# Feed-forwards ordered by a planner in the kernel, and a fourth quad in four gate/up blocks of each

## The chip, the cores and the metric

The kernel runs on one core of a Trainium2 chip. The metric is device time in microseconds (us) of one execution. TensorE is PE in the profile, its weight loads are PEld, VectorE is DVE, ScalarE is ACT, GpSimd is POOL, and SyncE is SP, which here only issues DMAs.

## What is computed

One block of a network over 256 tokens of width 2048: a gated feed-forward, a mixer (a recurrent branch and a pooling branch), and a second feed-forward, each behind a norm, with a norm on its result and a residual sum.

```python
D_MODEL, SEQ, D_FF = 2048, 256, 5632

def _swiglu(x, w_gate, w_up, w_down):
    return (jax.nn.silu(x @ w_gate) * (x @ w_up)) @ w_down

f = _swiglu(_rmsnorm(h, ln_ffn1_pre), ffn1_gate, ffn1_up, ffn1_down)
h = h + 0.5 * _rmsnorm(f, ln_ffn1_post)
mx = _hybrid_mixer(_rmsnorm(h, ln_mix_pre), w_in, ..., w_out)
h = h + _rmsnorm(mx, ln_mix_post)
f = _swiglu(_rmsnorm(h, ln_ffn2_pre), ffn2_gate, ffn2_up, ffn2_down)
h = h + 0.5 * _rmsnorm(f, ln_ffn2_post)
```

All inputs and the output are float32.

## The kernel before

**Products.** Every float32 operand is split into a high half, rounded to the type `F32R` that TensorE multiplies, and a low half, the rest. A product is three matmuls (`mm3`, lines 177 to 179): high times high, high times low, low times high. Activations lie transposed and split, 128 rows of k by 256 tokens; "h" is one of the two halves of 128 tokens. Weights come from memory in pieces of 128 rows of k (a k-tile) by 512 columns; ScalarE writes the high half and VectorE subtracts it from the raw weight to get the low half (lines 153 and 154 for plain pieces, 392 and 393 inside a quad). The split weights lie in a ring of `WS_BUFS` = 5 buffers of 1024 columns, the raw ones in `W32_BUFS` = 4. A pool of `NUNITS` = 33 buffers ("units") of 1024 columns holds everything longer-lived.

**Stages of a feed-forward.** Gate and up are made in eleven blocks of 512 columns over the 16 k-tiles; block 0 runs under another order, block 1 is plain, blocks 2 to 10 (`FAST`) go through `seven`. The result of a block is transposed in squares on VectorE, moved by 16 DMAs that POOL issues (`carry_at`, line 635), and split again (lines 647 and 651). Then the down projection runs over 44 k-tiles as two calls of `seven` with 1024 columns each (`post`), with a norm and the residual at the end; the last 16 k-tiles run one token half after the other (`by_half`). The mixer's out projection goes through `post` as well.

**Pairs and quads.** `seven` makes two column blocks at once (f and l: gate and up, or two neighbours of the down projection). A `pair` takes two k-tiles of one column block: four products, 12 matmuls. A `quad` takes two k-tiles of both column blocks and does with seven products (21 matmuls) what pairs do with eight. It needs sums of weights (`t13`, line 377; `t2`, line 381; `t4`, line 385), four splits (lines 392, 393), and sums of activations, which `sums` makes once per feed-forward (lines 268 to 317). Its partial products stand in banks of their own and are put together in `merge` (lines 416 and 419); `total` (line 435) adds what belongs to the second column block; lines 720, 724 and 623 are the gate's nonlinearity, the product and the transposition. A call with `n` quads takes 2n k-tiles out of both column blocks. Gate/up blocks have `NG` = 3 quads, after the third and fifth f pair and the second l pair (`SPOTS`).

**Order.** TensorE, ScalarE and VectorE run in the order in which the program emits their instructions. That order comes from a list of TensorE's work (`put`, each with its length) and events (`at`), which run when the sum of these lengths passes a time that is written by hand or taken from the ring (`slot`). SP and POOL are ordered by the framework's own scheduler.

Of the kernel before, what the change touches and what calls it, by code (L numbers as in the profile page):

```python
# [11 lines left out]
F32 = mybir.dt.float32  # L12
# [6 lines left out]
P = 128  # L19
# [23 lines left out]
AHEAD = (5.0, 6.0)  # L43
# [12 lines left out]
ROWS2 = [("r_k", 8), ("gn_w", 8), ("gn_b", 8), ("pool_scale", 8)]  # L56


class Block:
    def __init__(s, tc, ctx):  # L60
# [5 lines left out]
        s.late, s.after, s.items, s.events, s.now = [], [], deque(), [], 0.0  # L66
        s.clk, s.uses = 0.0, []
# [35 lines left out]
    def at(s, t, fn):  # L103

        s.n += 1
        heapq.heappush(s.events, (t, s.n, fn))

    def slot(s, end):

        s.uses.append(end)  # L110
        n = len(s.uses) - 1 - WS_BUFS
        return s.uses[n] if n >= 0 else n - 1.0

    def run(s):

        s.now = 0.0
        E = mybir.EngineType
        with s.tc.manual_schedule(engines={E.PE, E.Activation, E.DVE}):
            while s.items or s.events:
                while s.events and (s.events[0][0] <= s.now or not s.items):  # L120
                    heapq.heappop(s.events)[2]()
                if s.items:
                    t, fn = s.items.popleft()
                    fn()
                    s.now += t
            s.stats()
        s.now = s.clk = 0.0
        s.uses = []

    def put(s, t, fn):  # L130
        s.items.append((t, fn))
        s.clk += t
# [48 lines left out]
    def gemm_tok(s, w, c0, at, KT, evac, lead=False, trail=False, xs=None, hold=False,  # L181
# [19 lines left out]
        if trail:  # L201
            both(0, KT - TRAIL)
            s.by_half(w, c0, KT - TRAIL, KT, s.clk, AHEAD[0], do, keep,
                      lambda h: evac(h, pss[h]))
            return
        k0 = 0
        if xs:
            s.head(w, c0, KT, do, keep, xs)
            k0 = KT
        elif lead:  # L210
            s.by_half(w, c0, 0, STAG, s.clk, AHEAD[1], do, keep)
            s.run()
            k0 = STAG
        both(k0, KT)
        if hold:
            for h in range(2):
                s.at(0.3 + 1.6 * h, lambda h=h: evac(h, pss[h]))
            return
# [4 lines left out]
    def gemm_at(s, w, c0, at, KT, evac):  # L223

        pss = []
        ws = {}

        def load(k):
            ws.update((i, (wH, wL)) for i, wH, wL in s.load_w(w, k, 2, c0, 512))

        def do(k):
            if not pss:
                pss.extend(s.pm.tile([P, 512], F32, tag="mm", name=s.nm("mm"))
                           for _ in range(2))
            for h in range(2):
                (wH, wL), (xH, xL) = ws[k], at(k)
                s.mm3(pss[h], xH[:, h * P:h * P + P], xL[:, h * P:h * P + P], wH, wL,
                      k == 0, k == KT - 1)
        for k in range(0, KT, 2):
            s.at(s.slot(s.clk + 12 * MM), lambda k=k: load(k))  # L240
            s.put(6 * MM, lambda k=k: do(k))
            s.put(6 * MM, lambda k=k: do(k + 1))
        for h in range(2):
            s.at(s.clk + 0.3 + 1.6 * h, lambda h=h: evac(h, pss[h]))

    def by_half(s, w, c0, k0, k1, start, ahead, do, keep, done=None):

        for k in range(k0, k1, 2):
            s.at(start + (k - k0) * 3 * MM - ahead,
                 lambda k=k: keep(s.load_w(w, k, 2, c0, 512, k - k0 >= STAG)))  # L250
        for h in range(2):
            for k in range(k0, k1):
                s.put(3 * MM, lambda k=k, h=h: do(k, h))
            if done:
                s.put(0, lambda h=h: done(h))

    def sums(s, T, out, when, own=None, nq=2):

        nc = s.nc
        V = nc.vector  # L260
        tt = {}
        fl = lambda t: t.rearrange("p a b t -> p (a b t)")

        def first():
            xH, xL = [t[:, :2 * nq].bitcast(F32).rearrange("p k t -> p (k t)")
                      for t in T[len(out) // 2]]
# [15 lines left out]
        def parts():  # L282

            j = len(out) // 2
# [14 lines left out]
        def lows():  # L299
# [3 lines left out]
            for i in range(2):  # L303
                out.append([(s12[0][:, m, i], s12[1][:, m, i]) for m in range(2)]
                           + [tuple(u[:, i] for u in v) for v in (s3, s4)])
# [9 lines left out]
        def fourth():  # L315
            f, fH, fL = tt["f"], tt["H"], tt["L"]
            V.tensor_tensor(out=fl(fL), in0=fl(f), in1=fl(fH).bitcast(F32), op=ALU.subtract)
            for i in range(nq):
                out.append([(fH[:, m, i], fL[:, m, i]) for m in range(4)])
        for i, fn in enumerate((first, second) + ((parts, lows) if own is not None  # L320
                                                  else (third, fourth))):
            s.at(when + 1.7 * i, fn)

    def seven(s, wf, cf, wl, cl, at, KT, T, sm, n, spots, ev_first, ev_last, trail=0,
              one_end=False, ends=(-0.05, 2.7)):


        nc = s.nc
        V = nc.vector
        K0 = 2 * n  # L330

        bank = {}
        std = KT - K0
        left = dict(f0=std + n, f1=std, l0=std + n, l1=std + n, p1=n, p5=n, p6=n, p7=n)

# [16 lines left out]
        def pair(k, w, c0, b):  # L352
            s.at(s.slot(s.clk + 12 * MM), lambda: keep(s.load_w(w, k, 2, c0, 512)))
# [5 lines left out]
            s.put(12 * MM, do)  # L359

        def quad(q):
            k = 2 * q
            v, x = {}, {}
            a, b, c, d = [s.slot(s.clk + m * MM) for m in (6, 9, 15, 21)]

            def get():
                va, vb = [s.wp.tile([P, 1024], F32, tag="w32", name=s.nm("w32"),
                                    bufs=W32_BUFS).rearrange("p (a c) -> p a c", a=2)
                          for _ in range(2)]
                for dst, kk, w, c0 in ((va[:, 0], k, wl, cl), (vb[:, 0], k, wf, cf),  # L370
                                       (va[:, 1], k + 1, wf, cf), (vb[:, 1], k + 1, wl, cl)):
                    nc.sync.dma_start(out=dst, in_=w[kk * P:kk * P + P, c0:c0 + 512])
                v.update(a=va, b=vb[:, 1:], t13=s.unit((P, 2, 512), F32, "t13"),
                         t24=s.unit((P, 2, 512), F32, "t24"), b0=vb[:, :1])

            def t13():
                V.tensor_tensor(out=v["t13"], in0=v["a"],  # L377
                                in1=v["b0"].to_broadcast([P, 2, 512]), op=ALU.subtract)

            def t2():  # L380
                V.tensor_tensor(out=v["t24"][:, 0], in0=v["a"][:, 0], in1=v["t13"][:, 1],  # L381
                                op=ALU.add)

            def t4():
                V.tensor_tensor(out=v["t24"][:, 1], in0=v["b"][:, 0], in1=v["t24"][:, 0],  # L385
                                op=ALU.subtract)

            def split(n_, m):
                wH = s.wp.tile([P, 1024], F32R, tag="wH", name=s.nm("wH"), bufs=WS_BUFS)
                wL = s.wp.tile([P, 1024], F32R, tag="wL", name=s.nm("wL"), bufs=WS_BUFS)  # L390
                H, L = [t_[:, :m * 512].rearrange("p (a c) -> p a c", a=m) for t_ in (wH, wL)]
                nc.scalar.copy(H, v[n_])  # L392
                V.tensor_tensor(out=L, in0=v[n_], in1=H.bitcast(F32), op=ALU.subtract)  # L393
# [6 lines left out]
            s.put(6 * MM, lambda: (mul("p1", rows(k, 0), x["a"][0]),  # L400
                                   mul("f0", S_(4), x["a"][1])))
            s.put(3 * MM, lambda: mul("l0", rows(k + 1, 0), x["b"][0]))
            s.put(6 * MM, lambda: (mul("p5", S_(1), x["t13"][0]),
                                   mul("p7", S_(3), x["t13"][1])))
            s.put(6 * MM, lambda: (mul("p6", S_(2), x["t24"][0]),
                                   mul("l1", rows(k + 1, 1), x["t24"][1])))
        u = []

        gap = 0.1 if one_end else 1.4

        def merge():
            m = s.clk

            def start():
                u.extend(s.tmp("u") for _ in range(4))
                nc.scalar.copy(u[0], bank["p1"])

            def add(o, b, i):
                V.tensor_tensor(out=u[o], in0=bank[b], in1=u[i], op=ALU.add)  # L419
            s.merged = m + 0.7  # L420
# [1184 lines left out]
```

## Time and profile before

| | us |
|---|---|
| median of 3 runs | 2030.01 |
| lowest and highest of the runs | 2029.83, 2030.64 |
| profiled execution: span from its first to its last instruction | 2028.3 |
| PE busy | 2012.7 (99%) |
| DVE busy | 1746.8 (86%) |
| ACT busy | 1159.4 (57%) |
| mean granted TensorE clock | 0.998 |

The profile is of one execution; the page gives its span and no time of its own besides, so the runs stand beside it. A matmul's record is its latency, so TensorE's busy time says that it worked, not how densely. In a row of a timeline stand the start, the length, the engine, the line, the operation, the tiles that it writes and reads, the shapes, the count of merged neighbours and, in brackets, idle time before it with what ended it. In a row of waits stand who waited for whom, the total in us, how often, and the longest.

### The profile page before, as it was taken

How to read it: one execution, taken by the hardware profiler on the slowest of the kernel's cores; microseconds unless marked ns; L12 is line 12 of the kernel's file. 1: busy time of each engine (PE TensorE's matmuls, PEld its weight loads, DVE VectorE, ACT ScalarE, POOL GpSimd, SP SyncE). 2: the span in 40 equal slices, each digit the busy share in tenths (PEclk: the TensorE clock that was granted, in tenths of full speed). 3: DMA queues.
4: the chain of work that ended last, by engine and by line, in shares of the span. 5: the costliest groups of instructions: out<-in, count | busy, mean ns of one | idle time of the engine just before them, and what ended most of it. 6: DMA issues, size and time to landing. Idle time of an engine off the chain costs nothing.

```text
span 2028.3 us, 28794 instructions
## 1 busy us (share of the span) xinstructions
PE 2012.7 (99%) x10011; PEld 1664.0 (82%) x10011; DVE 1746.8 (86%) x2304; ACT 1159.4 (57%) x1559; POOL 323.4 (16%) x673
## 2 busy tenths in 40 slices
PE   9999999999999999999999999999999999999997
PEld 7888888888888888888788788888888888888886
DVE  6999999999998867799689577869999999999986
ACT  7555555555555566685576444565555555555553
POOL 0122111221000023413220111001211112110000
PEclk9999999999999999999999999999999999999999
DMA  7667676676667777757556558676676767666674
GB/s 261 192 207 224 218 219 207 209 222 213 197 218 258 224 213 211 203 177 215 148 171 186 160 169 274 206 220 193 202 226 211 227 200 227 217 208 203 213 258 146
DMA packets 226841, 423.55 MB, mean 209 GB/s; under 512 B 24063, under 2 KB 27529, under 8 KB 226697
## 3 DMA queue, kind: packets, MB, share of 16 engines
q1 hardware_dynamic: 204137, 384.70, 61.1%
q0 software_dynamic: 22272, 36.51, 5.5%
q8 instruction: 78, 1.28, 0.3%
q10 hardware_dynamic: 288, 0.52, 0.1%
q14 instruction: 66, 0.54, 0.1%
HBM read 396.69 MB, written 8.39 MB: 200 GB/s over the span
## 4 chain that ended last, share of the span: by engine, by line
PE 97%; issue 1%; DVE 1%; ACT 0%; POOL 0%; DMA 0%; POOLq 0%; DVEq 0%; SPq 0%; ACTq 0%
PE mm L177 27%; PE mm L179 27%; PE mm L178 27%; PE ms L177 4%; PE ms L178 4%; PE ms L179 4%; PE tr L605 1%; PE pA L1326 0%; PE mc L576 0%; PE pU L1422 0%; DMA w<-in_ffn_gate_dram 0%; PE pSa L1434 0%; PE pY L1457 0%; PE pT L1493 0%; PE pM L1392 0%
## 5 line engine op out<-in xcount | busy, mean ns | idle before, releaser
L177 PE MATMUL mm<-wH,xH 128*128 128x512 f32 (+1 forms) x2232 | 870.4, 391 | 0.0
L179 PE MATMUL mm<-wH,xL 128*128 128x512 f32 (+1 forms) x2232 | 866.2, 388 | 0.7 <-DVE xL L613 0.7
L178 PE MATMUL mm<-wL,xH 128*128 128x512 f32 (+1 forms) x2232 | 866.1, 388 | 0.0
L154 DVE TENSOR_TENSOR wL<-w,wH 128x1024 fp32r<-128x1024 f32 (+2 forms) x551 | 660.4, 1211 | 183.3 <-ACT wH L153 175.4
L153 ACT CAST wH<-w 128x1024 fp32r<-128x1024 f32 (+2 forms) x551 | 567.3, 1045 | 351.5 <-PE mm L179 241.9
L179 PEld LDWEIGHTS mm<-wH,xL 128*128 128x128 f32 x2232 | 419.0, 188 | 87.9 <-DVE xL L613 1.5
L177 PEld LDWEIGHTS mm<-wH,xH 128*128 128x128 f32 x2232 | 418.9, 188 | 86.9 <-issue 0.4
L178 PEld LDWEIGHTS mm<-wL,xH 128*128 128x128 f32 x2232 | 419.2, 188 | 83.9 <-DVE wL L154 0.3
L392 ACT CAST wH<-t 128x1024 fp32r<-128x1024 f32 x172 | 181.0, 1054 | 283.8 <-DVE t L385 180.0
L635 POOL DMA_DIRECT2D x<-T x352 | 172.3, 498 | 734.0 <-issue 401.1
L393 DVE TENSOR_TENSOR wL<-t,wH 128x1024 fp32r<-128x1024 f32 x172 | 209.9, 1223 | 11.1 <-ACT wH L392 6.6
L393 DVE TENSOR_TENSOR wL<-w,wH 128x1024 fp32r<-128x1024 f32 (+1 forms) x172 | 163.6, 951 | 1.1 <-ACT wH L392 1.1
L392 ACT CAST wH<-w 128x1024 fp32r<-128x1024 f32 (+1 forms) x172 | 140.4, 832 | 25.6 <-DMA w<-in_ffn_down_dram 13.5
L377 DVE TENSOR_TENSOR t<-w,w 128x1024 f32<-128x1024 f32 x86 | 105.0, 1220 | 2.3 <-DMA w<-in_ffn_down_dram 2.3
L179 PE MATMUL ms<-wH,sL 128*128 128x512 f32 x174 | 67.7, 389 | 0.0
L178 PE MATMUL ms<-wL,sH 128*128 128x512 f32 x174 | 67.7, 389 | 0.0
L177 PE MATMUL ms<-wH,sH 128*128 128x512 f32 x174 | 67.7, 389 | 0.0
L419 DVE TENSOR_TENSOR u<-ms,u 128x512 f32<-128x512 f32 x92 | 61.4, 687 | 1.4
L688 POOL DMA_DIRECT2D R<-R x96 | 47.0, 497 | 84.1 <-issue 72.2
L385 DVE TENSOR_TENSOR t<-w,t 128x512 f32<-128x512 f32 x86 | 59.1, 687 | 0.0
L381 DVE TENSOR_TENSOR t<-w,t 128x512 f32<-128x512 f32 x86 | 59.1, 687 | 0.0
L814 POOL DMA_DIRECT2D gb<-in_ln_ffn_post_dram x4 | 2.2, 557 | 285.0 <-PE mm L179 142.6
(323 smaller groups left out, 1986.1 us busy)
## 6 DMA issues: line engine op xcount, KB each, us to landing
w<-in_w_in_dram SPq DMA_DIRECT2D x128, 512.0 KB
w<-in_ffn_up_dram SPq DMA_DIRECT2D x122, 512.0 KB
w<-in_ffn_gate_dram SPq DMA_DIRECT2D x120, 512.0 KB
w<-in_ffn_down_dram SPq DMA_DIRECT2D x116, 512.0 KB
w<-in_ffn_down_dram SPq DMA_DIRECT2D x120, 256.0 KB
w<-in_ffn_gate_dram SPq DMA_DIRECT2D x112, 256.0 KB
w<-in_ffn_up_dram SPq DMA_DIRECT2D x108, 256.0 KB
w<-in_w_out_dram SPq DMA_DIRECT2D x28, 512.0 KB
```

The source lines that it names most:

```text
L153: s.nc.scalar.copy(vH, v)
L154: s.nc.vector.tensor_tensor(out=vL, in0=v, in1=vH.bitcast(F32), op=ALU.subtract)
L177: nc.tensor.matmul(ps, aH, bH, start=start, stop=False)
L178: nc.tensor.matmul(ps, aH, bL, start=False, stop=False)
L179: nc.tensor.matmul(ps, aL, bH, start=False, stop=stop)
L377: V.tensor_tensor(out=v["t13"], in0=v["a"], in1=v["b0"].to_broadcast([P, 2, 512]), op=ALU.subtract)
L381: V.tensor_tensor(out=v["t24"][:, 0], in0=v["a"][:, 0], in1=v["t13"][:, 1], op=ALU.add)
L385: V.tensor_tensor(out=v["t24"][:, 1], in0=v["b"][:, 0], in1=v["t24"][:, 0], op=ALU.subtract)
L392: nc.scalar.copy(H, v[n_])
L393: V.tensor_tensor(out=L, in0=v[n_], in1=H.bitcast(F32), op=ALU.subtract)
L419: V.tensor_tensor(out=u[o], in0=bank[b], in1=u[i], op=ALU.add)
L635: nc.gpsimd.dma_start(out=x[0][q * 32:q * 32 + 32, i], in_=src[i * 32:i * 32 + 32, q])
```

## The change

The hand-set times go. `Plan` collects every operation of the feed-forwards and of `post` as a node: engine, duration (`cost`), what it depends on, which buffers it takes and gives back, and for TensorE its place in time. `solve` derives due times backward from TensorE's places, then runs the list forward: at each step the engine whose next operation can start first gets the one that is due first. The program is emitted in that order; SP is now ordered by it too. A raw weight may take a unit where its four buffers are full. The order of pairs and quads is written as strings, in which f and l are pairs and q a quad. Blocks 3, 5, 7 and 9 have four quads; the other strings repeat the patterns of before. The activation sums for the third and fourth quad are made together (`SUMS`).

```diff
-AHEAD = (5.0, 6.0)
-DOWN = ((0, 7, ((8, 12), (0, 3, 5, 7, 9)), 0),
-        (2, 8, ((2, 4, 6, 8, 10, 12), (0, 2)), TRAIL))
-OUT = ((0, 0, (), 0), (1, 2, ((4,), (0,)), 0), (3, 0, (), TRAIL))
-FAST = range(2, 11)
-CARRY = (18, 21)
-NG, SPOTS = 3, ((2, 4), (1,))
+DOWN = ((0, "fffffffffqffffqff" "lqlllqllqllqllqlllll", 0),
+        (2, "fffqffqffqffqffqffqf" "lqllqlll", TRAIL))
+OUT = ((0, "", 0), (1, "fffffqf" "lqlllll", 0), (3, "", TRAIL))
+GATE_UP = ["", "ffffffffllllllll"] + ["fffqffqllqlll", "ffqfqfqlqlll"] * 4 + ["fffqffqllqlll"]
+SUMS = (2, 2)
+LAT = dict(PE=0.22, DVE=0.1, ACT=0.17, SP=0.0, POOL=8.0)
+UNITS = dict(ffn=25, out=22)
+FIFO = dict(pt=4, pm=4, tmp=TB)
+SPARE, KEEP, URGENT = 3, 4, 8.0
+SOON, LATEST, BEFORE = 22.0, 12.0, 12.0
+EARLY = 0.5
+RATE, LEAVE, LAND = 0.25, 1.05, 2.0
...
+def cost(eng, n, extra=0.0):
+    return extra + (n / 960 + 0.068 if eng == "DVE" else n / 1200 + 0.095)
...
+    def solve(s):
...
+        for n in reversed(s.nodes):
+            for m in succ[n]:
+                if n.eng == "PE":
+                    break
+                v = m.due - n.dur - (n.lat + (EARLY if m.eng == "PE" else 0.0)
+                                     if m.eng != n.eng else 0.0)
+                n.due = v if n.due is None else min(n.due, v)
+            if n.due is None:
+                n.due = n.born + LATEST
...
+        while len(order) < len(s.nodes):
+            best = None
+            for e, c in front.items():
+                got = [(when(n), n) for n in c]
+                if got:
+                    first = min(a for a, _ in got)
+                    a, n = min((x for x in got if x[0] <= first + 1e-9),
+                               key=lambda x: x[1].due)
+                    if best is None or a < best[0]:
+                        best = (a, n)
...
+            if n.size:
+                line = max(n.free + LEAVE, line) + n.size / RATE
+                n.end = max(n.end, line + LAND)
...
     def run(s):
...
-        with s.tc.manual_schedule(engines={E.PE, E.Activation, E.DVE}):
-            while s.items or s.events:
...
+        with s.tc.manual_schedule(engines={E.PE, E.Activation, E.DVE, E.SP}):
+            for n in s.plan.solve():
+                n.fn()
             s.stats()
...
+    def fetch(s, w, k, c0, keep, hold=False):
+
+        p, x = s.plan, {}
+        src = Tok("w32", "unit")
+        dst = [Tok("unit"), Tok("unit")] if hold else [Tok("ring")]
...
+        n = p.op("SP", 0.4, load, take=[src], size=0.52, chain="SP")
+        n = p.op("ACT", cost("ACT", 1024), cast, [n], take=dst, chain="cast")
+        return p.op("DVE", cost("DVE", 1024), low, [n], rel=[src]), dst
...
         def quad(q):
...
-            for t, fn in ((a, get), (a, t13), (a, lambda: split("a", 2)), (a, t2),
-                          (b, lambda: split("b", 1)), (b, t4), (c, lambda: split("t13", 2)),
-                          (d, lambda: split("t24", 2))):
-                s.at(t, fn)
...
+            ld = [p.op("SP", 0.4, lambda m=m: get(m), take=([ka], [kb], (), ())[m], size=0.26,
+                       chain="SP") for m in range(4)]
...
+            one, two = cost("DVE", 512), cost("DVE", 1024)
+            n13 = p.op("DVE", two, t13, ld[:3], [k13, k24], [ka, kb])
+            la, ra = half("a", 2, [ld[0], ld[2]], [ka])
+            n2 = p.op("DVE", one, t2, [n13], (), [ka, k13])
+            lb, rb = half("b", 1, [ld[3]], [kb])
+            n4 = p.op("DVE", one, t4, [n2, ld[3]], (), [kb])
+            l13, r13 = half("t13", 2, [n13], [k13])
+            l24, r24 = half("t24", 2, [n4], [k24])
...
+            p.pe(6 * MM, lambda: (mul("p1", rows(k, 0), x["a"][0]),
+                                  mul("f0", S_(4), x["a"][1])),
+                 [la, ds, dep(k)] + claim("p1", "f0", "f1"), ra)
+            p.pe(3 * MM, lambda: mul("l0", rows(k + 1, 0), x["b"][0]),
+                 [lb] + claim("l0", "l1"), rb)
+            p.pe(6 * MM, lambda: (mul("p5", S_(1), x["t13"][0]),
+                                  mul("p7", S_(3), x["t13"][1])),
+                 [l13] + claim("p5", "p7"), r13)
+            d = p.pe(6 * MM, lambda: (mul("p6", S_(2), x["t24"][0]),
+                                      mul("l1", rows(k + 1, 1), x["t24"][1])),
+                     [l24] + claim("p6"), r24)
...
         def ev_of(c):
...
     def ffn(s, wg, wu, wd, uT, rs, gpost, resid, emit, reload, xs=None):
...
+            s.seven(wg, b * 512, wu, b * 512, x, dep, NKD, need, su, GATE_UP[b], ev_f, ev_l, {})
...
+        s.post(wd, s.T_at(hT), NKF, gpost, 0.5, resid, emit, reload, hT, hTd, sm, DOWN, hTk)
```

More of the change, by code (lines that the diff above doesn't have):

```diff
@@ new lines, in add, with merge @@
+        def add(o, b, i):
+            if u[o] is None:
+                new(o)
+            V.tensor_tensor(out=u[o], in0=bank[b], in1=u[i], op=ALU.add)
+        m, use = {}, {}
+        def merge(d):
+            for i in range(4):
+                use[i] = p.claim("tmp")
+            m["u0"] = p.op("ACT", cost("ACT", 512), copy, [d] + use[0][0])
+            held["p1"].append(m["u0"])
+            d = m["u0"]
+            for o, b, i in ((1, "p6", 0), (2, "p7", 1), (1, "p5", 1), (3, "p5", 2)):
+                d = m[f"u{o}"] = p.op("DVE", one, lambda o=o, b=b, i=i: add(o, b, i),
+                                      [d] + (use[o][0] if o > 1 or b == "p6" else []))
+                held[b].append(d)
+                use[i][1].append(d)
@@ L758, in ffn, with turned, ev_g @@
[L758 to L762 removed]
+        one = cost("DVE", 512)
+        sig = {}
+        T1 = [[] for _ in range(nb)]
+        def turned(b, h, src):
+            if not T1[b]:
+                T1[b].append(s.unit(p="T1"))
+            s.turn(T1[b][0], h, src)
+        def ev_g(b, h, ps):
+            sig[b, h] = s.tmp("sg")
+            nc.scalar.activation(out=sig[b, h], in_=ps, func=AF.Silu, scale=rs[h])
@@ new lines, in ffn, with carry @@
+        p = s.plan
+        p.units = UNITS["ffn"]
+        for _ in range(2):
+            p.claim("pm")
+        k1 = Tok("unit")
+        last = p.begin
+        for h in range(2):
+            last = p.op("DVE", one * 2, lambda h=h: up(h), [last], [k1] if h == 0 else ())
+            for r in ("pm", "tmp"):
+                p.claim(r)[1].append(last)
+        hTd, hTk = [], []
+        def carry(b, turned, k1):
+            n, k = s.carry(T1[b], hT, turned, k1)
+            hTd.append(n)
+            hTk.append(k)
```

812 lines of the change are left out of this document (509 added, 303 removed).

## The prediction

> **What bounds the kernel now.** I read the page first: the engines' shares and the 40 slices.
>
> ```profile
> span 2028.3 us, 28794 instructions
> ...
> PE 2012.7 (99%) x10011; PEld 1664.0 (82%) x10011; DVE 1746.8 (86%) x2304; ACT 1159.4 (57%) x1559; POOL 323.4 (16%) x673
> ...
> PE   9999999999999999999999999999999999999997
> ...
> DVE  6999999999998867799689577869999999999986
> ```
>
> TensorE is busy in every slice, and VectorE is nearly full in the slices of the two feed-forwards (about 1 to 14 and 27 to 39), not in the mixer between them. A busy PE need not be a fed PE, so the next view is the list of TensorE's waits over the whole span.
>
> ```profile
> PE warm L484 <- POOL ident masks.py:199: 1.7, 1, 1.7
> PE mm L179 <- DVE xL L613: 0.7, 2, 0.5
> PE pS L1442 <- ACT R L1436: 0.7, 1, 0.7
> PE tr L605 <- DVE fg L846: 0.7, 1, 0.7
> PE tr L605 <- DMA x<-in_x_dram: 0.5, 1, 0.5
> ```
>
> That is the complete list: 4.3 us, none of it inside a feed-forward's gate/up or down blocks (the L613 rows are in the first 10 us, the L846 row is the joint to the mixer). So in the feed-forwards the time is the number of matmuls times their distance. The distance is read from two rows of TensorE's timeline inside a block, nine steps apart:
>
> ```profile
> 140.81 0.39 PE L179 MATMUL mm<-wH,xL 128*128 128x512 f32 x1
> ...
> 142.85 0.39 PE L179 MATMUL mm<-wH,xL 128*128 128x512 f32 x1
> ```
>
> 2.04 us over 9 steps are 0.2267 us for one matmul (the 0.39 is a pipelined latency). A gate/up block with three quads has 192 - 9 = 183 matmuls, so 41.5 us. The view by stage, cut at a block's length, agrees (columns: PE, PEld, DVE, ACT, POOL busy with counts, PE clock, DMA share, GB/s):
>
> ```profile
> 140.40:181.80 41.40, 41.40 (x184) 34.32 (x183) 39.56 (x46) 23.56 (x28) 7.81 (x16) 1.00 0.70 216
> 181.80:223.30 41.50, 41.50 (x184) 34.36 (x183) 39.80 (x46) 23.70 (x28) 7.82 (x16) 1.00 0.69 216
> ```
>
> The second carrier of these blocks is VectorE at 39.8 of 41.5 us. Its own timeline over one block, 181.34 to 222.73, prices all its parts:
>
> ```profile
> 181.34 1.21 DVE L154 TENSOR_TENSOR wL<-w,wH 128x1024 fp32r<-128x1024 f32 x1
> 182.47 1.22 DVE L377 TENSOR_TENSOR t<-w,w 128x1024 f32<-128x1024 f32 x1
> 183.61 1.22 DVE L393 TENSOR_TENSOR wL<-w,wH 128x1024 fp32r<-128x1024 f32 x1
> 184.74 0.69 DVE L381 TENSOR_TENSOR t<-w,t 128x512 f32<-128x512 f32 x1
> 185.34 1.28 DVE L435 TENSOR_TENSOR u<-mm,u 128x512 f32<-128x512 f32 x2
> 186.54 1.29 DVE L724 TENSOR_TENSOR u<-u,u 128x512 f32<-128x512 f32 x2
> 187.74 1.30 DVE L623 STREAM_TRANSPOSE T<-u 128x512 f32<-128x512 f32 x2
> ...
> 204.03 1.22 DVE L377 TENSOR_TENSOR t<-w,w 128x1024 f32<-128x1024 f32 x1
> 205.16 1.22 DVE L393 TENSOR_TENSOR wL<-w,wH 128x1024 fp32r<-128x1024 f32 x1
> 206.30 0.69 DVE L381 TENSOR_TENSOR t<-w,t 128x512 f32<-128x512 f32 x1
> 206.90 0.69 DVE L393 TENSOR_TENSOR wL<-w,wH 128x512 fp32r<-128x512 f32 x1
> 207.50 0.69 DVE L385 TENSOR_TENSOR t<-w,t 128x512 f32<-128x512 f32 x1
> 208.10 2.51 DVE L393 TENSOR_TENSOR wL<-t,wH 128x1024 fp32r<-128x1024 f32 x2
> 210.53 0.69 DVE L651 TENSOR_TENSOR xL<-x,xH 128x512 fp32r<-128x512 f32 x1
> 211.72 1.23 DVE L154 TENSOR_TENSOR wL<-w,wH 128x1024 fp32r<-128x1024 f32 x1 [0.51 <-ACT wH L153]
> 213.19 2.36 DVE L154 TENSOR_TENSOR wL<-w,wH 128x1024 fp32r<-128x1024 f32 x2 [0.24 <-ACT wH L153]
> ...
> 217.74 1.23 DVE L154 TENSOR_TENSOR wL<-w,wH 128x1024 fp32r<-128x1024 f32 x1 [0.45 <-ACT wH L153]
> 218.88 2.73 DVE L419 TENSOR_TENSOR u<-ms,u 128x512 f32<-128x512 f32 x4
> 221.53 1.28 DVE L419 TENSOR_TENSOR u<-mm,u 128x512 f32<-128x512 f32 x2
> 222.73 1.21 DVE L154 TENSOR_TENSOR wL<-w,wH 128x1024 fp32r<-128x1024 f32 x1
> ```
>
> The starts matter, not the durations: successive operations overlap. 182.47 to 184.74 is two operations of 1024 columns, so 1.135 us each; 184.74 to 185.34 and its like give 0.60 us for 512 columns. A pair (two k-tiles of one weight) costs VectorE one 1.135. A quad (two k-tiles of both weights) costs four of 1.135 (L377, three L393) and three of 0.60 (L381, L385, one L393): 6.34 us. A block's ends are 14 of 0.60 (two L435, two L724, two L623, two L651, six L419): 8.40 us. Three quads, ten pairs and the ends make 19.02 + 11.35 + 8.40 = 38.77 us of the 41.4 us between the first and the last row; 2.6 us are left, of which 0.51 + 0.24 + 0.45 = 1.20 us are marked waits for ScalarE.
>
> **The change part by part.** *The fourth quad.* A quad needs 7 products of three matmuls where its pairs need 8: 21 for 24. Blocks 3, 5, 7 and 9 of each feed-forward gain one quad, so 8 x 3 = 24 matmuls go: 24 x 0.2267 = 5.44 us. These lie on the path that sets the end, as TensorE waits for nothing there. The down blocks and the out projection have the same pattern written as a string as before (7, 8 and 2 quads after the same pairs), block 1 has the same eight and eight pairs, so their matmuls do not change.
>
> *What it costs VectorE.* Each fourth quad adds 6.34 and removes two pairs: 6.34 - 2.27 = +4.07 us, to 42.84 us, while TensorE's block shrinks to 180 x 0.2267 = 40.8 us. Such a block alone is over-full by 2.0 us. With its three-quad neighbour it is 81.61 us of VectorE in 82.3 us of TensorE: 0.7 us free in two blocks. This is the number on which all hangs. The place where it is tightest is the middle of the new block, the sequence quad, pair, quad, pair, quad, pair, quad: a quad and a pair are 33 matmuls, 7.48 us, and 6.34 + 1.135 = 7.48 us of VectorE, exactly as much. Over that stretch TensorE takes 4 x 4.76 + 3 x 2.72 = 27.2 us and VectorE 28.8 us, plus 3.6 us of ends of the block before (L435, L724, L623). Against the start of the last product, VectorE must enter the block some 2 to 3 us ahead. The split weights lie in a ring of five buffers: five halves of 1.135 us, and the 2.3 us of L377, L381 and L385 that use no ring buffer, so a lead of up to about 6 us can be stored (an estimate from these rows). It fits, with nothing over.
>
> *The order.* Before, a quad's sums wait at a hand-set time; the rows at 211.72 and 217.74 show VectorE idle with the next quad's L377, which needs no ring buffer, still behind in its queue. After, whatever is ready goes first, so that idle time can be filled with L377 to L385 of the next quad. What VectorE loses otherwise is shown by these answers for 140.4 to 472.6:
>
> ```profile
> DVE wL L154 <- ACT wH L153: 11.4, 26, 1.6
> ACT wH L153 <- DMA w<-in_ffn_gate_dram: 16.2, 11, 2.8
> ACT wH L153 <- PE mm L179: 3.7, 12, 0.4
> ```
>
> 11.4 us in eight blocks is 1.4 us each; part of it comes from weights that landed late. The change lets raw weights also use free units beside the four buffers and fixes SP's order too, so loads can be issued earlier. The bounds for what is left of it: nothing, or 1.2 us in every block as now. I take nearly nothing, because an engine that is behind its supply always has something ready, and in these pairs VectorE is behind.
>
> *Small parts.* The fourth quad needs sums for two k-tiles where one was made: the costs double from half size, three times 0.535 us, 1.6 us of VectorE once per feed-forward, covered by the 2.6 us of block 2; uncovered it would cost 1.6 us twice. ScalarE gets three and a half casts for two, +1.6 us on 23.7 of 41.5: hidden, and if not hidden it shows up as the waits just listed. SP issues four loads of 256 KB for two of 512 KB with the same bytes; DMA is at 0.69 to 0.70 of its engines: hidden, and if not, a wait of up to the 2.8 us above. POOL's 16 moves per block stay. The joint to the mixer keeps its turn times, so its 0.7 us stays; at best it goes.
>
> *The sum.* The profile gives a span of 2028.3 us and no other time for that execution; the runs' median is 2030.01, 1.7 us more, which I carry over unchanged. 2030.0 - 5.4 = 2024.6; for the exactly full stretches I allow TensorE waits of about 0.6 us in all (some 0.08 us in each of eight blocks), so 2025.2.
>
> Here a rule of the Trainium skill stands against the change: "VectorE: DVE Perf Modes" gives an fp32 sum of N columns (N+151)/0.96 ns (in the section on the TRN2 errata), an estimate of 1.22 and 0.69 us for these sizes, and says under "The DRAIN you can't avoid" that the next operation does not start until the pipe is empty. The durations in the trace agree with the formula (1.22 and 0.69), the starts do not agree with the drain (1.135 and 0.60).
>
> **The rivals.** *VectorE stays as idle as it is (the other side).* If the ring, not the order, makes the waits of 1.20 us, each pair of blocks needs 81.61 + 2.40 = 84.0 us against 82.96 now: +1.05 us, eight times, +8.4: 2038.4 us, bound by VectorE. It decides from 1.35 us of idle per pair on (82.96 - 81.61). For it: the 2.43 us from 208.10 to 210.53 contain 0.16 us of waiting inside a quad, and seven of these are already 1.1 us. Against: that wait is there because nothing else was queued between.
>
> *Half of it.* With 1.20 us of idle per pair: 82.81, so -0.15 us eight times: 2028.8 us, no change.
>
> *Loads or joints go wrong.* SP's order is now fixed by an assumed transfer rate in the down blocks and across the joints too. If a wait such as the 2.8 us one reaches TensorE once in each gate/up half and each down half, four times: 2030.0 - 5.4 + 11.2 = 2035.8 us.
>
> *Operations of VectorE that cannot overlap.* By durations, a three-quad block is 10 x 1.22 + 3 x 6.95 + 14 x 0.69 = 42.7 us and a four-quad block 47.2 us; a pair of blocks would be 89.9, +6.9 eight times, 2085 us. But 42.7 is already more than the 41.5 us in which the trace runs a block without a wait of TensorE, so this is next to excluded. It is what the drain of the Trainium skill's VectorE page would make of it.
>
> **How the numbers follow.** What can be told from no change in this kernel is about 0.2%, 4 us. TensorE stays fed: 0.57, 2025.2 us. Half: 0.18. VectorE bound: 0.18. Loads or joints: 0.06. No overlap: 0.01. Faster by over 0.2% is the first case, 0.57; within 0.2% the second, 0.18; slower the last three, 0.25. The likeliest case's own range is 2023.6 (the joint's 0.7 us gone and none of the allowance used) to 2026.0. The range that holds 8 in 10 must reach over both middle cases to the VectorE-bound one: 2023.6 to 2038.4.
>
> **What would show it.** Right: 24 matmuls fewer in the feed-forwards; the list of TensorE's waits as short as now; blocks 3, 5, 7, 9 at about 40.8 us and their neighbours at 41.5 us; VectorE's marked waits in those pairs under 0.7 us, with L377's successors moved ahead into the ends of blocks. Wrong: entries "PE mm <- DVE wL" of 1 us and more around the third or fourth quad, and blocks of 42 us and over; or ScalarE's casts waiting for DMA at the head of a down block.

## The result and the profile after

| | before | after |
|---|---|---|
| median of 11 runs, us | 2030.52 | 2025.53 |
| lowest and highest, us | 2029.83, 2031.56 | 2025.22, 2026.46 |
| span of the profiled execution, us | 2028.3 | 2023.6 |
| matmuls and transposes on PE | 10011 | 9987 |

The ratio is 0.9975, with a 95% interval of 0.9966 to 0.9984. The forecast was 2025.2 us.

The head of the page after, and TensorE's complete list of waits:

```profile
span 2023.6 us, 28609 instructions
...
PE 2008.3 (99%) x9987; PEld 1660.2 (82%) x9987; DVE 1774.4 (88%) x2344; ACT 1180.8 (58%) x1575; POOL 325.2 (16%) x673
...
DVE  6999999999989857799689577779999999999896
```

```profile
PE warm L698 <- POOL ident masks.py:199: 1.7, 1, 1.7
PE mm L315 <- DVE xL L840: 1.6, 4, 0.5
PE pS L1789 <- ACT R L1783: 0.7, 1, 0.7
PE mm L313 <- ACT xH L831: 0.4, 2, 0.2
```

24 matmuls are gone, and no wait of TensorE stands in a gate/up block. Blocks with four quads are called dense here, the others plain. The view by stage, cut at the starts of blocks 2, 3, 4 and 5 (columns as before: length, then PE, PEld, DVE, ACT and POOL busy):

```profile
98.86:140.34 41.48, 41.48 (x184) 34.35 (x183) 41.31 (x49) 24.46 (x28) 7.82 (x16) 1.00 0.63 216
140.34:181.14 40.80, 40.80 (x181) 33.78 (x180) 40.63 (x48) 25.11 (x27) 7.81 (x16) 1.00 0.72 243
181.14:222.62 41.48, 41.48 (x184) 34.35 (x183) 41.20 (x48) 22.66 (x25) 7.82 (x16) 1.00 0.53 173
222.62:263.42 40.80, 40.80 (x181) 33.78 (x180) 40.70 (x48) 26.87 (x31) 7.82 (x16) 1.00 0.58 189
```

The dense blocks take 40.80 us and their neighbours 41.48, and VectorE goes from 39.8 of 41.5 us to 40.6 to 41.3. Its waits for ScalarE in blocks 3 to 10, which were 11.4 us in 26 pieces over eight blocks, are now one row:

```profile
DVE wL L370 <- ACT wH L367: 2.5, 3, 1.5
```

Its timeline inside block 3 shows where they went. Lines 550, 555 and 559 are the weight sums (377, 381 and 385 before), 572 the low halves in a quad (393), 370 those of a pair (154):

```profile
143.44 0.68 DVE L559 TENSOR_TENSOR t<-w,t 128x512 f32<-128x512 f32 x1
144.04 1.21 DVE L550 TENSOR_TENSOR t<-w,w 128x1024 f32<-128x1024 f32 x1
145.18 1.22 DVE L572 TENSOR_TENSOR wL<-t,wH 128x1024 fp32r<-128x1024 f32 x1
146.31 0.68 DVE L555 TENSOR_TENSOR t<-w,t 128x512 f32<-128x512 f32 x1
147.03 0.69 DVE L559 TENSOR_TENSOR t<-w,t 128x512 f32<-128x512 f32 x1
147.63 1.22 DVE L370 TENSOR_TENSOR wL<-w,wH 128x1024 fp32r<-128x1024 f32 x1
...
174.93 2.73 DVE L619 TENSOR_TENSOR u<-ms,u 128x512 f32<-128x512 f32 x4
177.57 1.28 DVE L619 TENSOR_TENSOR u<-mm,u 128x512 f32<-128x512 f32 x2
```

The next quad's first sum (144.04) now runs before the last low half of the one at hand (145.18). Before, the two last low halves of a quad stood one behind the other, and the second started late (2.43 us for two from 208.10 on). The marked waits before stood at the low halves of pairs.

The lengths of the stages, counted from first matmul to first matmul, for all runs below. "Gate/up" is blocks 2 to 10; "mixer" ends and "joint" begins at the second feed-forward's first matmul; "joint" ends at that feed-forward's block 1. The stages are those of the profiled execution, which in hand4 was 3.9 us and in evens 1.4 us longer than the median.

| run | median us | gate/up 1 | mixer | joint | gate/up 2 |
|---|---|---|---|---|---|
| before | 2030.5 | 373.7 | 621.9 | 45.46 | 373.3 |
| after | 2025.5 | 370.6 | 622.2 | 46.60 | 370.6 |
| three | 2035.0 | 373.3 | 625.8 | 46.64 | 373.3 |
| ffn2three | 2028.8 | 370.6 | 622.2 | 46.61 | 373.3 |
| hand4 | 2057.3 | 389.4 | 621.9 | 45.46 | 388.7 |
| five | 2027.0 | 371.3 | 622.2 | 46.61 | 371.2 |
| nine | 2058.2 | 378.1 | 626.1 | 46.59 | 378.0 |
| evens | 2029.1 | 371.9 | 622.6 | 45.46 | 370.9 |
| raw4 | 2040.0 | 375.4 | 622.2 | 50.96 | 375.3 |
| dose1 | 2031.5 | 372.7 | 622.2 | 46.61 | 373.6 |
| dose2 | 2047.3 | 375.5 | 625.8 | 46.61 | 376.9 |
| joint | 2026.8 | 370.6 | 624.7 | 45.46 | 370.6 |
| joint2 | 2024.3 | 370.6 | 622.2 | 45.46 | 370.6 |

Between before and after the spans differ by 4.7 us: 2 x 2.72 us for the quads, another 0.36 in blocks 9 and 10 of the first feed-forward (41.67 and 41.65 us before, now 40.80 and 41.48), and 0.4 us at the end behind the last matmul; against that 1.14 us more at the joint and 0.3 in the mixer.

### The profile page after: what moved, and what is told of

Read it like the earlier page. It is cut to its first block, busy times and chain, and to the rows that moved or that the text cites. A ratio compares the mean times of both kernels' runs of the same rounds, so it can differ in the third digit from the quotient of the medians.

```text
span 2023.6 us, 28609 instructions
## 1 busy us (share of the span) xinstructions
PE 2008.3 (99%) x9987; PEld 1660.2 (82%) x9987; DVE 1774.4 (88%) x2344; ACT 1180.8 (58%) x1575; POOL 325.2 (16%) x673
## 4 chain that ended last, share of the span: by engine, by line
PE 98%; issue 1%; DVE 1%; ACT 0%; DMA 0%; DVEq 0%; POOLq 0%; POOL 0%; SPq 0%; ACTq 0%
PE mm L313 27%; PE mm L315 27%; PE mm L314 27%; PE ms L313 4%; PE ms L315 4%; PE ms L314 4%; PE tr L822 0%; PE pA L1673 0%; PE mc L790 0%; PE pU L1769 0%; DMA w<-in_ffn_gate_dram 0%; PE pSa L1781 0%; PE pY L1804 0%; DVE xL L840 0%; PE pT L1840 0%
## 5 line engine op out<-in xcount | busy, mean ns | idle before, releaser
L313 PE MATMUL mm<-wH,xH 128*128 128x512 f32 (+1 forms) x2184 | 851.5, 391 | 0.4 <-ACT xH L831 0.4
L315 PE MATMUL mm<-wH,xL 128*128 128x512 f32 (+1 forms) x2184 | 847.8, 388 | 1.6 <-DVE xL L840 1.6
L314 PE MATMUL mm<-wL,xH 128*128 128x512 f32 (+1 forms) x2184 | 847.5, 388 | 0.0
L367 ACT CAST wH<-w 128x1024 fp32r<-128x1024 f32 x333 | 346.8, 1053 | 239.7 <-PE mm L315 209.2
L370 DVE TENSOR_TENSOR wL<-w,wH 128x1024 fp32r<-128x1024 f32 x333 | 396.9, 1217 | 39.5 <-ACT wH L367 36.5
L290 DVE TENSOR_TENSOR wL<-w,wH 128x1024 fp32r<-128x1024 f32 (+2 forms) x202 | 239.0, 1192 | 96.5 <-ACT wH L289 93.3
L289 ACT CAST wH<-w 128x1024 fp32r<-128x1024 f32 (+2 forms) x202 | 207.7, 1034 | 164.5 <-PE mm L315 142.9
L313 PE MATMUL ms<-wH,sH 128*128 128x512 f32 x252 | 98.0, 389 | 0.0
L314 PE MATMUL ms<-wL,sH 128*128 128x512 f32 x252 | 98.0, 389 | 0.0
L315 PE MATMUL ms<-wH,sL 128*128 128x512 f32 x252 | 98.0, 389 | 0.0
```

The costliest lines, as they stand in the source:

```text
L289: s.nc.scalar.copy(vH, v)
L290: s.nc.vector.tensor_tensor(out=vL, in0=v, in1=vH.bitcast(F32), op=ALU.subtract)
L313: nc.tensor.matmul(ps, aH, bH, start=start, stop=False)
L314: nc.tensor.matmul(ps, aH, bL, start=False, stop=False)
L315: nc.tensor.matmul(ps, aL, bH, start=False, stop=stop)
L367: s.nc.scalar.copy(x["H"], x["v"])
```

## The experiments

The medians of before, measured again beside these runs, lay between 2030.4 and 2031.1 us.

**three: the new order with three quads.**

```diff
-GATE_UP = ["", "ffffffffllllllll"] + ["fffqffqllqlll", "ffqfqfqlqlll"] * 4 + ["fffqffqllqlll"]
+GATE_UP = ["", "ffffffffllllllll"] + ["fffqffqllqlll"] * 9
```

> The new order with three quads in every gate/up block (24 matmuls put back). If the gain is the 24 matmuls and nothing else, each of blocks 3, 5, 7 and 9 is 41.48 us again and the time is 2025.5 + 5.4 = 2031.0 us, a little above the kernel before, because the joint before the second feed-forward lost about 1.1 us in the new order. Rival: the order itself brings the gain (no idle VectorE, earlier loads, shorter tail), and the time stays at 2025.5 to 2028 us.

Measured 2035.0 us, ratio to before 1.0022 (1.0013 to 1.003). The blocks are as the first theory has them, 41.48 us each; the rival falls. But 4 us are over what was expected, and 3.6 of them lie in the mixer, where nothing was edited: 625.8 for 622.2 us. TensorE's waits in its window 880 to 940, where the kernel after has none from 870 to 930:

```profile
PE pA L1673 <- DVE R L1649: 1.2, 2, 1.0
PE pB L1692 <- DVE R L1684: 1.1, 2, 0.8
PE mm L313 <- ACT sgb L1309: 0.6, 1, 0.6
```

VectorE runs the recurrence's operations in another order there. That order is not in the list: the framework's scheduler makes it, and it can come out differently when the feed-forward ahead of it does (in five, dose1 and raw4 the mixer kept its 622.2 us). "nine", "joint" and "dose2" wait at the same two lines. So totals of these runs can't be compared alone; the stages can.

**ffn2three: the same in the second feed-forward alone.** Nothing ahead of the mixer changes.

```diff
-            s.seven(wg, b * 512, wu, b * 512, x, dep, NKD, need, su, GATE_UP[b], ev_f, ev_l, {})
+            s.seven(wg, b * 512, wu, b * 512, x, dep, NKD, need, su,
+                    GATE_UP[b] if xs or b < 2 else GATE_UP[2], ev_f, ev_l, {})
```

> The changed kernel with three quads in all blocks of the second feed-forward, the first one as changed. Everything ahead of the second feed-forward is the same, so the mixer should not move. If a fourth quad is worth its 3 matmuls, the time is 2025.5 + 4 x 0.68 = 2028.2 us, with blocks of 41.48 us. Rival: part of the gain is the order in these blocks, and the time is 2026 to 2027 us.

Measured 2028.8 us, 0.999 (0.9981 to 0.9999). The mixer stays at 622.2, the second feed-forward's blocks take 373.3 for 370.6 us: 2.7 us for four quads, 0.68 us each.

**hand4: the fourth quad under the hand-set times.** The kernel before with:

```diff
+NG4, SPOTS4 = 4, ((1, 2, 3), (0,))
...
-                s.sums(st["nT"], st["su"], s.clk + 27, nq=1)
+                s.sums(st["nT"], st["su"], s.clk + 27)
...
-                s.seven(wg, b * 512, wu, b * 512, s.T_at(nT), NKD, nT, su, NG, SPOTS,
-                        ev_f, ev_l, one_end=True)
+                four = b in (3, 5, 7, 9)
+                s.seven(wg, b * 512, wu, b * 512, s.T_at(nT), NKD, nT, su,
+                        NG4 if four else NG, SPOTS4 if four else SPOTS,
+                        ev_f, ev_l, one_end=True)
```

> The kernel before with its hand-set times, and a fourth quad in blocks 3, 5, 7 and 9 (sums for the fourth quad added). If the order is what makes room on VectorE, its 1.2 us of waits per block stay, VectorE becomes the bound, TensorE shows waits for wL in these blocks, and the time is 2030.8 to 2038.4 us (2030.0 + 1.05 us for each of eight pairs of blocks at most; 2030.8 if half the waits go). Rival: the order is not needed, the weights split ahead cover it, and the time is 2024.6 to 2026 us.

Measured 2057.3 us, 1.013 (1.0114 to 1.0145): with the hand-set times as they were, the fourth quad costs 26.9 us instead of gaining, far more than the 8.4 us over before that I had as a bound. Other hand-set times were not tried. Blocks 3, 4 and 10 by stage, TensorE's waits over the run, and one of VectorE's in blocks 3 to 10:

```profile
140.35:183.87 43.52, 41.66 (x182) 33.33 (x180) 42.60 (x50) 24.17 (x29) 7.81 (x16) 1.00 0.66 204
183.87:225.54 41.67, 41.67 (x183) 34.38 (x184) 40.52 (x47) 24.67 (x29) 7.82 (x16) 1.00 0.70 217
441.96:488.24 46.28, 43.55 (x184) 35.19 (x185) 40.45 (x47) 24.22 (x29) 7.83 (x16) 0.96 0.62 200
```

```profile
PE mm L178 <- DVE u L420: 11.2, 8, 2.0
PE ms L179 <- DVE wL L394: 7.0, 10, 1.3
PE mm L179 <- DVE wL L394: 4.7, 2, 2.8
```

```profile
DVE t L382 <- DMA x<-T: 4.7, 1, 4.7
```

About half of this waiting is not for weights. VectorE's additions that free a result bank (line 420) stand, at their hand-set time, behind the splits of the dense block, and the next block can't start: 11.2 us, once behind every dense block. The weights make 11.7 us. The longest of these (2.0 and 2.8 us) fall in block 10 of each feed-forward, a plain one. There VectorE stood idle for 4.7 and 5.5 us in front of a quad's sum (line 382), by the trace for the transfers of the carry, the transposed result of an earlier block. So hand4 shows more than one thing that the old times did not allow for, and not all of it is VectorE's work.

**nine, five and evens: more quads, and other places.** "nine" has `["ffqfqfqlqlll"] * 9`, "five" the dense string in block 10 too, "evens" (on top of joint2, below) in blocks 2, 4, 6, 8 and 10.

```diff
-GATE_UP = ["", "ffffffffllllllll"] + ["fffqffqllqlll", "ffqfqfqlqlll"] * 4 + ["fffqffqllqlll"]
+GATE_UP = ["", "ffffffffllllllll"] + ["ffqfqfqlqlll"] * 9
...
+GATE_UP = ["", "ffffffffllllllll"] + ["fffqffqllqlll", "ffqfqfqlqlll"] * 4 + ["ffqfqfqlqlll"]
...
+GATE_UP = ["", "ffffffffllllllll"] + ["ffqfqfqlqlll", "fffqffqllqlll"] * 4 + ["ffqfqfqlqlll"]
```

> The new order with four quads in all nine blocks 2 to 10. If VectorE's 42.84 us per such block against 40.80 us of TensorE is the limit, nine blocks are 18.4 us over-full; what the stages at both ends can take (5.1 us free in block 1, 6.8 us in the first down half) is at most 12 us, so 6 to 18 us are lost per feed-forward against a saving of 3.4 us: 2031 to 2055 us, with TensorE waiting for wL. Rival: VectorE's room is larger than its starts say, TensorE stays fed, and the time is 2025.5 - 6.8 = 2018.7 us.

Measured 2058.2 us, 1.0136 (1.0122 to 1.0149), 3 us above the range; the longer mixer, which the range left out, is 3.9 us of it. Blocks 3 and 8 by stage:

```profile
140.36:181.16 40.80, 40.80 (x182) 33.80 (x180) 40.59 (x48) 25.59 (x29) 7.70 (x16) 1.00 0.57 197
349.05:391.45 42.40, 41.83 (x181) 33.42 (x180) 42.19 (x49) 24.13 (x28) 7.35 (x15) 1.00 0.68 214
```

Blocks 2 to 4 still run at TensorE's pace on what was stored. Blocks 5 and 6 take 41.7 and 43.1 us, 7 to 9 take 42.4 us each, and 10 takes 43.8. In 7 to 9 VectorE starts 24 operations of 1024 columns and 24 of 512 in each, without a wait. The 42.84 us that were counted have 26 of 512: two (the carry's low halves, 1.2 us) are put off, and starts that follow one another more slowly than counted add 0.7 us. The first down halves pay for what was put off: 121.1 and 122.6 us instead of 114.9.

> The new order with a fourth quad in block 10 as well (five of nine blocks). Block 10 has 2.3 us of VectorE free, the first down half behind it 6.8 us; the fourth quad takes 4.07 us and shortens the block by 0.68 us. If work can be put off into the down half, the time is 2025.5 - 1.36 = 2024.2 us. Rival: the block is closed on its own, 2.4 us over-full less what is free, and the time is 2026 to 2030 us.

Measured 2027.0 us, 0.9983 (0.9975 to 0.9992). Block 10, behind a dense block, takes 42.13 us instead of 41.48 or 40.80: the rival holds, 0.65 us lost against a plain block in each feed-forward.

> Four quads in blocks 2, 4, 6, 8 and 10 (five instead of four), the joint before the second feed-forward as in the run that changes it alone. The blocks alternate as before, but the stretch begins and ends with a full one. If what is free in block 1 (5.1 us) and in the first down half (6.8 us) carries both ends, the time is 2024.4 - 1.4 = 2023.0 us. Rival: VectorE has only about 0.1 us free per pair (as the doses showed) and enters block 2 without a lead, so blocks 2 to 10 lose 1 to 3 us per feed-forward: 2025 to 2029 us. A mixer that falls into the other order adds 2.5 to 4 us to either; then the blocks' lengths decide.

Measured 2029.1 us, 0.9992 (0.9983 to 1.0). The rival again: blocks 6 to 9 lose 1.9 us in the first and 1.0 in the second feed-forward, and the first down halves take 116.4 us for 114.9. (In the first feed-forward VectorE also waited once, 2.4 us in block 7, for a weight that landed late.) Four, placed as they are, is the most that these tries found.

**dose1 and dose2: how much room VectorE has.** In blocks 3, 5, 7 and 9 one operation of 1.135 us is repeated once or twice.

```diff
+            for _ in range(1 if KT == NKD and order.count("q") == 4 and q == 0 else 0):
+                n13 = p.op("DVE", two, again, [n13], (), [ka, kb])
             la, ra = half("a", 2, [ld[0], ld[2]], [ka])
```

> The changed kernel with VectorE's first sum of the first quad (1.135 us, the same result again) made twice in each of blocks 3, 5, 7 and 9. If VectorE has only the 0.65 us per pair of blocks that were counted beforehand, each of eight pairs loses about 0.5 us: 2029.4 us. Rival, from the trace of the changed kernel: work moved over the edges of the stretch leaves about 8.9 us free in blocks 2 to 9, four doses are 4.5 us, and the time stays at 2025.5 us with blocks of 40.80 and 41.48 us.

> As the single dose, but made three times in all: 2.27 us more of VectorE in each of blocks 3, 5, 7 and 9, 9.1 us per feed-forward. With 0.65 us free per pair each of eight pairs loses 1.6 us: 2038.5 us. With 8.9 us free in blocks 2 to 9 the dose just fills them: 2025.5 to 2030 us, the loss in the last pairs.

Measured 2031.5 us (1.0004, 0.9995 to 1.0013) and 2047.3 us (1.0081, 1.0065 to 1.0096). dose1, blocks 3, 7 and 9, then dose2, blocks 3 and 6 to 9:

```profile
140.92:181.72 40.80, 40.80 (x182) 33.77 (x180) 40.59 (x47) 24.41 (x26) 7.87 (x16) 1.00 0.66 225
305.48:347.23 41.75, 41.46 (x181) 33.33 (x180) 41.54 (x48) 24.16 (x28) 3.23 (x7) 1.00 0.57 189
388.84:430.36 41.52, 41.35 (x181) 33.47 (x180) 41.31 (x48) 23.39 (x27) 0.07 (x1) 1.00 0.57 179
```

```profile
140.69:181.49 40.80, 40.80 (x181) 33.78 (x180) 40.59 (x48) 24.57 (x27) 7.58 (x16) 1.00 0.62 205
264.23:305.80 41.57, 41.57 (x184) 34.42 (x184) 41.36 (x48) 24.50 (x29) 12.41 (x26) 1.00 0.69 229
305.80:348.68 42.88, 41.97 (x181) 33.24 (x180) 42.60 (x49) 24.15 (x28) 3.23 (x7) 1.00 0.54 175
348.68:390.26 41.58, 41.58 (x183) 34.43 (x184) 41.37 (x48) 22.93 (x27) 12.41 (x26) 1.00 0.68 217
390.26:433.14 42.88, 41.93 (x182) 33.25 (x180) 42.60 (x49) 22.75 (x26) 0.02 (x1) 1.00 0.65 210
```

Three rows from the first feed-forward of dose2 show how long a dose is (550 is the sum, 554 its repetitions):

```profile
389.71 1.22 DVE L550 TENSOR_TENSOR t<-w,w 128x1024 f32<-128x1024 f32 x1
390.97 2.48 DVE L554 TENSOR_TENSOR t<-w,w 128x1024 f32<-128x1024 f32 x2
393.37 1.22 DVE L576 TENSOR_TENSOR wL<-w,wH 128x1024 fp32r<-128x1024 f32 x1
```

Blocks 3 and 4 lose nothing. Later, a dense and a plain block, a pair that should take 82.28 us, take 42.88 + 41.58 = 84.46 in dose2, 2.18 us more for a dose of 2.27; in dose1 the last two pairs of the first feed-forward lose 1.07 and 1.02 us of 1.135. That would be a room of about 0.1 us in a steady pair. But a repetition writes the same sum again and starts 1.26 us after the one before it, as the rows show, so these doses are 2.51 and 1.26 us, and the room is 0.2 to 0.3 us. Beside it there is a store. Counted at 1.135 us each, dose1 gives 4.5 us per feed-forward and loses 2.1 us in the first and 3.0 in the second, so 2.4 and 1.5 us are absorbed. In dose2 part of the loss comes later: the first down halves take 117.6 us for 114.9. With them, 7.6 of 9.1 us are lost in the first feed-forward and 9.0 in the second.

Both runs lie above either theory: 2031.5 for 2029.4 and 2047.3 for 2038.5 us. The first theory had too much room and left out the down halves and, for dose2, the longer mixer (3.6 us). My second theory, 8.9 us free, falls as well. In the full blocks 6 to 10 of dose2, in which VectorE waits for nothing, its starts still lie 0.8 to 0.9 us per block further apart than 1.135 and 0.60 us each would make, so such distances are not room. Two of VectorE's groups in blocks 7 and 8 of dose2 show where the room comes from (854 is the transposition of a result, 888 a carry's low half, 623 and 651 before):

```profile
L854 DVE STREAM_TRANSPOSE T<-u 128x512 f32<-128x512 f32 x4 | 2.8, 709 | 0.1
L888 DVE TENSOR_TENSOR xL<-x,xH 128x512 fp32r<-128x512 f32 x2 | 1.3, 670 | 0.0
```

Each block has two of either, so two low halves of four are put off. They are not needed before the down projection.

**raw4: raw weights in their four buffers only.**

```diff
-        src = Tok("w32", "unit")
+        src = Tok("w32")
...
-            ka, kb = Tok("w32", "unit"), Tok("w32", "unit")
+            ka, kb = Tok("w32"), Tok("w32")
```

> The changed kernel, with raw weights in their four buffers only (no units beside them). If VectorE's lead through the dense blocks rests on raw weights that arrive early, blocks 3, 5, 7 and 9 grow by 0.5 to 2 us each, with waits for wL: 2029.5 to 2042 us. Rival: the order alone carries it, four buffers are enough as they were for three quads, and the time is 2025.5 us.

Measured 2040.0 us, 1.0042 (1.0029 to 1.0056). The dense blocks grow by 1.0 to 1.5 us each and the joint by 4.4 us. ScalarE's waits for landing weights (blocks 3 to 10) come back; first raw4, then after:

```profile
ACT wH L367 <- DMA w<-in_ffn_gate_dram: 15.5, 12, 1.9
...
ACT wH L567 <- DMA w<-in_ffn_gate_dram: 10.5, 13, 1.9
```

```profile
ACT wH L367 <- DMA w<-in_ffn_gate_dram: 2.6, 3, 1.7
```

The order alone does not carry the dense blocks; it needs the earlier loads as well.

**joint and joint2: the joint before the second feed-forward.** "joint" lists the ten k-tiles there one by one, "joint2" does so at the second joint alone.

```diff
-                d = p.pe(6 * MM, lambda k=k, h=h: (do(k, h), do(k + 1, h)),
-                         [low, *deps, *at],
-                         dst if h else ())
+                if ready is not None and s.joints == 2:
+                    p.pe(3 * MM, lambda k=k, h=h: do(k, h), [low, *deps, *at])
+                    d = p.pe(3 * MM, lambda k=k, h=h: do(k + 1, h), (), dst if h else ())
+                else:
+                    d = p.pe(6 * MM, lambda k=k, h=h: (do(k, h), do(k + 1, h)),
+                             [low, *deps, *at],
+                             dst if h else ())
```

(In "joint" the test is `ready is not None` alone; `s.joints` counts the joints.)

> The changed kernel with the first products behind a joint (the ten k-tiles that run one token half after the other) listed one k-tile at a time instead of two, so that the transposes of the second half can fall between the last two k-tiles of the first half, as in the kernel before. If the 1.1 us that the joint before the second feed-forward lost comes from 16 transposes in a row with their splits behind them, the time is 2025.5 - 1.0 = 2024.5 us and the waits for xL at that joint go. Rival: the wait only moves, the transposes then wait for the residual sum (fg) as the kernel before did at the first joint, and the time stays at 2025.5 us.

> The finer list of products at the joint before the second feed-forward alone; everything ahead of that joint is as in the changed kernel. The run with both joints shortened this joint by 1.14 us (46.60 to 45.46) but its mixer took 2.5 us more. If that came from another order of the mixer's VectorE and ScalarE work, which follows from what is listed ahead of it, the mixer is 622.2 us again and the time is 2025.5 - 1.1 = 2024.4 us. Rival: the longer mixer belongs to the finer list itself, and the time is 2026 to 2027 us.

TensorE's timeline at the joint, after and then joint2:

```profile
1329.21 0.40 PE L315 MATMUL mm<-wH,xL 128*128 128x512 f32 x1
1329.45 1.91 PE L822 MATMUL tr<-ident,fg 128*128 128x128 f32 x16
1331.54 0.50 PE L313 MATMUL mm<-wH,xH 128*128 128x512 f32 x1 [0.18 <-ACT xH L831]
1331.88 0.39 PE L314 MATMUL mm<-wL,xH 128*128 128x512 f32 x1
1332.70 0.50 PE L315 MATMUL mm<-wH,xL 128*128 128x512 f32 x1 [0.43 <-DVE xL L840]
```

```profile
1328.78 0.60 PE L828 MATMUL tr<-ident,fg 128*128 128x128 f32 x4
...
1329.91 1.47 PE L828 MATMUL tr<-ident,fg 128*128 128x128 f32 x12
1331.14 0.48 PE L314 MATMUL mm<-wH,xH 128*128 128x512 f32 x1
```

With pieces of two k-tiles all 16 transposes fall behind the first half's last piece, and the second half waits for their splits. With single k-tiles four of them go three matmuls earlier, their splits run meanwhile, and the waits are gone: both runs have 45.46 us for 46.60. "joint" still measured 2026.8 us (0.998, 0.9971 to 0.9989), since its mixer fell into the longer order, 624.7 us. "joint2" leaves everything ahead as it was, and its mixer takes 622.2: **2024.3 us**, 0.9971 (0.9961 to 0.9982), 1.2 us better by the medians than the changed kernel. It is the best of all runs.

## Why the prediction was right

**The gain.** 24 matmuls at 0.2267 us were forecast, 5.44 us; ffn2three and the blocks' lengths show exactly 0.68 us per quad. It held because the list of TensorE's waits has none in these blocks, before or after; "three" shows that the new order without the fourth quad leaves them at 41.48 us.

**VectorE's room.** This number was too large. Forecast were 0.7 us in two blocks; the doses show 0.2 to 0.3, and that only because work is put off. The forecast took every start as independent of the one before. Where an addition needs the one right before it, the next start comes 0.72 us later, not 0.60. In a merge this is so twice: its four additions take 2.65 us, not 2.40, as the rows at 218.88 and 221.53 before said already. It is so for the sums at 555 and 559 where they run one behind the other (146.31 to 147.03). In blocks 7 and 8 of dose2 all seven quads have them so, 0.84 us; with the merges and some others it comes to 1.4 us without the doses. The 81.6 us that were counted for a pair of blocks are then 83.0, 0.7 more than TensorE's 82.28. What makes up for it are the two low halves that are put off, 1.2 us. That leaves 0.5 us by this sum, somewhat more than the doses show. The changed kernel uses the same way out: 8 low halves of the carry stand in the first 60 us behind block 10 of its first feed-forward, 2 before. So "it fits, with nothing over" came true by a way that the prediction did not name, which is luck; a fifth quad in any place tried cost more than it gave.

**The lead.** VectorE was said to need a lead of 2 to 3 us and to be able to store about 6. (The terms named there, five halves of 1.135 us and 2.3 us, add up to 8.0.) dose1 shows a store of 1.5 to 2.4 us beyond what the dense blocks use; dose2, with its down halves, 1.5 and 0.1. raw4 shows that it does not hold without the units for raw weights. I named these in half a sentence and gave them no price; without them the change is a loss, 2040.0 us.

**The order.** "I take nearly nothing" for VectorE's waits was right, 11.4 us became 2.5.

**The rival on the other side** fell, as VectorE's waits went. hand4 shows what the fourth quad costs where they stay (8.7 us for ScalarE in its blocks 3 to 10), and there the price was wrong: 2038.4 us forecast, 2057.3 measured. It counted these waits and no others. Banks that came free late, VectorE's stop in block 10 and, behind the longest stalls, TensorE's clock came on top.

**Small parts.** The first joint kept its wait, as said (0.4 and 0.2 us for splits in the place of 0.67 for the residual). The second joint, which had none, got 1.14 us: this step was missed, because the turn times were read as unchanged while the pieces between which they are placed had grown from three matmuls to six. The 0.6 us that were allowed for waits in dense blocks were not needed there; they were about what the joint and the mixer took (1.14 and 0.3), less what blocks 9, 10 and the tail gave back (0.36 and 0.4). So it is luck that the total is nearer to the forecast than its parts. The lower end of the likeliest case, 2023.6 us, is 2023.9 by its own terms (2024.6 less 0.7).

**The drain.** The Trainium skill's page "VectorE: DVE Perf Modes" says in the section "The DRAIN you can't avoid" that the next operation does not start until the pipe is empty, and at the end of the same paragraph that one which is not held starts earlier. Here independent operations start 1.135 and 0.60 us apart at lengths of 1.22 and 0.69 us, so the first of these statements does not give their distance. An addition that needs the result of the one right before it starts 0.72 us after it, behind its end.

What stays open: what ahead of the mixer makes the framework choose the longer order of its VectorE work. That it happens is shown by four runs, not why.

## What to carry to other kernels

When two engines are nearly full, add up the second one's starts, dependent operations apart from independent ones, before adding work to it; then feed it small doses, see where the loss begins, and look at what is put off and who pays for it later. A planned order is worth most together with the buffers that let its loads run ahead, and a change of the grain in which a list is written moves things that have times of their own. Where part of a program is ordered by a scheduler that sees what comes before, compare runs stage by stage.

## What the runs showed of the hardware

TensorE's clock fell to half after one idle stretch of 2.6 us. In raw4 a matmul starts at 1333.14 and the next 2.86 us later, 2.63 us more than the usual distance; from 1336.83 on eight matmuls start 0.427 us apart instead of 0.227. The granted clock (the third column from the end):

```profile
1330.00:1334.00 4.00, 3.53 (x16) 2.60 (x14) 3.31 (x6) 2.24 (x4) 1.31 (x3) 1.00 0.78 210
1334.00:1338.00 4.00, 2.00 (x6) 1.54 (x7) 3.74 (x5) 0.00 (x0) 1.46 (x3) 0.85 0.84 277
1338.00:1342.00 4.00, 4.00 (x22) 3.29 (x21) 0.00 (x0) 1.14 (x5) 0.00 (x0) 0.73 0.87 291
```

So this stall of VectorE cost TensorE about 1.6 us (8 x 0.2) more than the stall. In the feed-forwards of hand4, nine and dose2 the long steps from one matmul to the next divide in the same way: those of 2.34, 2.39, 3.16, 3.66 and 3.71 us were followed, within 2.4 us of their end, by 5 to 12 matmuls 0.43 us apart (1.0 to 2.4 us lost); those of 2.19 and 2.04 us and the shorter ones were not. The 2.34 us are in hand4's block 10 and had a step of 1.17 us right behind them. This is one reason why that block took 46.28 us (clock 0.96 in its row above).
